# Sample attention of a hybrid layer: plain fp32 in four column groups of TensorE, two sequences at a time

## The chip, the cores and the metric

One core of a Trainium2 chip runs the program. The metric is the device time of one execution in microseconds (us); the time of the kernel before is the median of three runs.

## The reference, cut to what matters

One layer of a decoder is computed for a prompt of 1024 tokens and for 8 sample sequences of 8 new tokens each, which share all weights. The part that the change touches is the attention of the samples. Each sequence has 1024 past tokens in 8 pages of 128, picked by `page_table` from a pool of 80 pages, plus its own 8 new tokens; there are 8 heads of 64.

```python
def fox_attend(q, k, v, cq, ck, qpos, kpos):
    s = jnp.einsum('bqhd,bkhd->bhqk', q, k).astype(jnp.float32) * ATT_SCALE
    s = s + jnp.swapaxes(cq, 1, 2)[..., None] - jnp.swapaxes(ck, 1, 2)[:, :, None, :]
    mask = kpos[None, :] <= qpos[:, None]
    p = jax.nn.softmax(jnp.where(mask, s, -jnp.inf), axis=-1)
    return jnp.einsum('bhqk,bkhd->bqhd', p.astype(v.dtype), v)

def fox_sample(q, k, v, logf, k_past, v_past, logf_past, pos):
    k_all = jnp.concatenate([k_past.astype(k.dtype), k], axis=1)
    v_all = jnp.concatenate([v_past.astype(v.dtype), v], axis=1)
    c_all = jnp.cumsum(jnp.concatenate([logf_past, logf], axis=1), axis=1)
    ...
```

## The kernel before, in words

All 1088 tokens (1024 of the prompt, then 64 of the samples) go through the projections together, transposed, 128 channels at a time. The kernel keeps fp32 accuracy in two ways. Most matmuls split each operand into a high part in fp32r and a rest (`wh`, `wl`, `hh`, `hl`), and take three matmuls (`mm3`, L171). A few are plain fp32 (the tiles `py`, `ph` and `pi` of the state-space stage, L735, L725 and L755): the trace shows each of those as two TensorE records.

The stages follow each other: normalisation, pooling, prompt attention, the state-space scan, sample attention, then the output projections. In each stage `interleave` (L196) mixes the main work with side work, so that TensorE has something while the main work waits. The side work of the sample stage is 13 of the 24 merge gates (`gate_steps`, L217): a gate is 72 matmuls in 6 steps of 12, on weights that arrive in two halves (`raw<-w`, SP), are rounded by ScalarE (`wh`, L166) and subtracted by GpSimd (`wl`, L167). `issue_after` holds a gate step behind the main step that lies `LAG[3]` steps back. Within that, the scheduler of the tile framework fixes the order of every engine's queue at build time, the order of the DMA issues on SP among them.

The sample stage is L881 to L1064. `load_k` (L908) fetches the keys of one sequence in four tiles `kr` of two pages, `load_v` (L918) the values in eight tiles `vr` of one page. For each sequence `b`:

- `scores(b)` (L926): every key tile is rounded by ScalarE into `kh` (L943), and VectorE or GpSimd write the rest `kl` (L944). The queries stand in `QB` as high and low parts. For each of four head pairs one matmul takes 128 columns of the array (high and low queries, both heads) with `kh`, and one takes 64 columns with `kl`. All four head pairs add into the same PSUM rows; high and low rows are added later.
- `softmax(b)` (L966) adds the decay row `ck`, takes the minimum, exponentiates into `T` (64 rows: 8 heads by 8 queries) and scales.
- `values(b)` (L1001): `T` is transposed in 8 pieces and split (`PT`), the values are split like the keys (`vh` L997, `vl` L998), and each page takes a matmul of 128 columns with `vh` and one of 64 columns with `vl`, each on all 512 value channels. Four transposes of `ol` pick out each head's own channels.

`samples` (L1045) runs `scores(0)`, `softmax(0)`, `scores(1)` and then, for each `b`, `values(b)` with `softmax(b + 1)` and `scores(b + 2)` mixed in. After the stage come the last three gates (L1066) and the output projections, all on TensorE.

Of the kernel before, what the change touches and what calls it, by code (L numbers as in the profile page):

```python
# [8 lines left out]
F = mybir.dt.float32  # L9
# [13 lines left out]
LAG = (99, 99, 40, 60)  # L23
# [4 lines left out]
def _tiles():  # L28
# [28 lines left out]
C_ID, C_M30, C_CBM, C_EL, C_CBS, C_ELS, C_INV, C_MB, C_MB7, C_CA8, C_SGN, C_MT, C_N = (  # L57
    0, 128, 256, 384, 512, 576, 640, 704, 712, 720, 728, 730, 734)


def kernel_body(ctx, tc, d):
# [65 lines left out]
    vsm = const.tile([64, 4, 128], F, name="vsm")  # L127
# [21 lines left out]
    lfD = dt_([8, NT], "lfD")  # L149
    ckD = dt_([64, 1032], "ckD")  # L150
    ckqD = dt_([8, 8, 8, 1032], "ckqD")
# [133 lines left out]
    def fd_chain():  # L285
# [40 lines left out]
        SP.dma_start(out=lfD, in_=e[0:8, :])  # L326
# [50 lines left out]
        for b in range(8):  # L377
            SP.dma_start(out=lg[b * 8:b * 8 + 8, 1024:1032], in_=lfD[:, 1024 + b * 8:1032 + b * 8])
# [5 lines left out]
        SP.dma_start(out=ckqD, in_=ckD.rearrange("(b h o) s -> b h o s", b=8, o=1).to_broadcast([8, 8, 8, 1032]))  # L384
# [59 lines left out]
    with ExitStack() as px:  # L444
# [101 lines left out]
        def vz(j):  # L546
# [5 lines left out]
            def v_done():  # L552
                SP.dma_start(out=d["o_v"][j], in_=vf)
                for i0 in (0, 4):
                    ps = psa()
                    for i in range(4):
                        PE.transpose(ps[:, i * 128:(i + 1) * 128], vf[:, (i0 + i) * 128:(i0 + i + 1) * 128], ident)
                    pv = ps.rearrange("p (i e x) -> p i e x", i=4, e=2)
                    S.copy(VS[:, i0:i0 + 4, :, 0:64], pv)
                    V.tensor_tensor(VS[:, i0:i0 + 4, :, 64:128], pv, VS[:, i0:i0 + 4, :, 0:64].bitcast(F), op=SUB)  # L560
                ps = psa()
                PE.transpose(ps[0:64, 0:128], vf[:, 1024:1088], ident)
                V.tensor_copy(vsm[:, j, :], ps[0:64, 0:128])
# [316 lines left out]

    with ExitStack() as px:  # L881
        a1 = px.enter_context(tc.tile_pool(name="a1", bufs=1))
        a2 = px.enter_context(tc.tile_pool(name="a2", bufs=2))
        a3 = px.enter_context(tc.tile_pool(name="a3", bufs=3))
        a4 = px.enter_context(tc.tile_pool(name="a4", bufs=4))
        a5 = px.enter_context(tc.tile_pool(name="a5", bufs=5))
        QB = [a1.tile([128, 576], R, name=f"QB{x}") for x in range(2)]
        Pn = [a1.tile([64, 64], F, name=f"Pn{x}") for x in range(2)]
        for x in range(2):
            V.memset(QB[x].bitcast(F), 0.0)  # L890
        ysm = a1.tile([128, 4, 64], F, name="ysm")
        vnh = a1.tile([64, 512], R, name="vnh")
        vnl = a1.tile([64, 512], R, name="vnl")
        vflat = vsm.rearrange("p j x -> p (j x)")
        S.copy(vnh, vflat)
        V.tensor_tensor(vnl, vflat, vnh.bitcast(F), op=SUB)
        knh = a1.tile([128, 4, 64], R, name="knh")
        knl = a1.tile([128, 4, 64], R, name="knl")
        S.copy(knh, ksm)
        V.tensor_tensor(knl, ksm, knh.bitcast(F), op=SUB)  # L900
        pages, kraw, vraw, score, soft = {}, {}, {}, {}, {}

        def page_of(b, p):
            if (b, p) not in pages:
                pages[b, p] = page(b, p)
            return pages[b, p]

        def load_k():  # L908

            for b in range(8):  # L910
                for u in range(4):
                    kraw[b, u] = kr = a5.tile([128, 4, 256], F, tag="kr", name="kr")
                    for p in range(2):
                        page_dma(out=kr[:, :, p * 128:p * 128 + 128],
                                 in_=d["ck"][bass.ds(page_of(b, 2 * u + p), 1)].rearrange("o p c s -> (o p) c s"))
                    yield

        def load_v():  # L918

            for b in range(8):  # L920
                for p in range(8):
                    vraw[b, p] = vr = a4.tile([128, 512], F, tag="vr", name="vr")
                    page_dma(out=vr, in_=d["cv"][bass.ds(page_of(b, p), 1)].rearrange("o s x -> (o s) x"))
                    yield

        def scores(b):  # L926

            bs = slice(b * 8, b * 8 + 8)
            qb = QB[b % 2]
            qv = qb.rearrange("p (h x) -> p h x", x=144)  # L930
            for e in range(2):
                p = slice(64 * e, 64 * e + 64)
                S.copy(qv[p, :, 8 * e:8 * e + 8], qsm[p, :, bs])
                V.tensor_tensor(qv[p, :, 64 + 8 * e:72 + 8 * e], qsm[p, :, bs],
                                qv[p, :, 8 * e:8 * e + 8].bitcast(F), op=SUB)
            pss = score[b] = [psa(f"s{n}") for n in range(3)]

            def split(u):
                keys(1)
                kr = kraw.pop((b, u))  # L940
# [4 lines left out]
                return kh, kl  # L945

            def products(ps, kh, kl):
# [6 lines left out]
            ahead = [split(0)]  # L954
            yield
            ahead.append(split(1))
            products(pss[2][:, 0:8], knh[:, :, bs], knl[:, :, bs])
            yield
            for u in range(4):
                kh, kl = ahead.pop(0)  # L960
                products(pss[u // 2][:, u % 2 * 256:u % 2 * 256 + 256], kh, kl)
                if u < 2:
                    ahead.append(split(u + 2))
                yield

        def softmax(b):  # L966

            bs = slice(b * 8, b * 8 + 8)
            pss, pn = score.pop(b), Pn[b % 2]
            ck = a1.tile([64, 1032], F, tag="ck", name="ck")  # L970
            SP.dma_start(out=ck, in_=ckqD[b].rearrange("h q s -> (h q) s"))
            V.tensor_tensor(ck[:, 1024:1032], ck[:, 1024:1032], cst[0:64, C_CA8:C_CA8 + 8], op=ADD)
            T = a2.tile([64, 1032], F, tag="T", name="T")
            mn = a2.tile([64, 4], F, tag="mn", name="mn")
            for n in range(3):
                w = 512 if n < 2 else 8
                sl = slice(n * 512, n * 512 + w)
                V.tensor_tensor(ck[:, sl], ck[:, sl], pss[n][64:128, 0:w], op=ADD)
                V.tensor_tensor_reduce(out=T[:, sl], in0=pss[n][0:64, 0:w], in1=ck[:, sl], scale=1.0,
# [8 lines left out]
            V.tensor_copy(pn[:, bs], T[:, 1024:1032])  # L988
            soft[b] = T, pn
            yield  # L990

        def split_v(b, p):
            next(vload, None)
            vr = vraw.pop((b, p))
            vh = a3.tile([128, 512], R, tag="vh", name="vh")
            vl = a3.tile([128, 512], R, tag="vl", name="vl")
            S.copy(vh, vr)  # L997
            (G if p % 2 else V).tensor_tensor(vl, vr, vh.bitcast(F), op=SUB)  # L998
            return vh, vl

        def values(b):  # L1001

            bs = slice(b * 8, b * 8 + 8)
            T, pn = soft.pop(b)
            PT = a2.tile([128, 8, 128], R, tag="PT", name="PT")
            PTn = a1.tile([64, 128], R, tag="PTn", name="PTn")
            ps = psa()
            for p in range(8):
                PE.transpose(ps[:, p * 64:p * 64 + 64], T[:, p * 128:p * 128 + 128], ident[0:64, 0:64])
            pv = ps.rearrange("p (c x) -> p c x", x=64)  # L1010
            S.copy(PT[:, :, 0:64], pv)
            V.tensor_tensor(PT[:, :, 64:128], pv, PT[:, :, 0:64].bitcast(F), op=SUB)  # L1012
            ps = psa()
            PE.transpose(ps[0:64, 0:64], pn, ident[0:64, 0:64])
            S.copy(PTn[:, 0:64], ps[0:64, 0:64])
            V.tensor_tensor(PTn[:, 64:128], ps[0:64, 0:64], PTn[:, 0:64].bitcast(F), op=SUB)
            ahead = [split_v(b, 0), split_v(b, 1)]
            yield
            po = psa("po")
            for p in range(8):  # L1020
                vh, vl = ahead.pop(0)
                if p < 6:
                    ahead.append(split_v(b, p + 2))
                PE.matmul(out=po, lhsT=PT[:, p, :], rhs=vh, start=(p == 0), stop=False)
                PE.matmul(out=po[0:64], lhsT=PT[:, p, 0:64], rhs=vl, start=False, stop=False)
                yield
            PE.matmul(out=po[0:64], lhsT=PTn[:, 0:64], rhs=vnl, start=False, stop=False)
            PE.matmul(out=po, lhsT=PTn, rhs=vnh, start=False, stop=True)
# [267 lines left out]
```

## Time and profile before

| | |
|---|---|
| runs | 1471.38, 1471.22 and 1466.72 us; median 1471.22 |
| profiled execution | 1468.5 us, span 1466.7 us |
| TensorE | matmul busy 96% of the span, weight loads 91% |
| VectorE, ScalarE, GpSimd | busy 53%, 42%, 37% |
| mean granted clock of TensorE | 0.985 |
| sample stage, first to last matmul | 885.7 to 1132.5 us of the span |

Times inside the execution are microseconds from the start of the span. A group of instructions is read as line, engine, operation, and output<-inputs; its shape is that of the moving operand, and 128*64 before it means 128 rows by 64 columns of the array. Matmuls are pipelined, so what one costs in a stream is the distance between two starts and not its duration.

### The profile page before, as it was taken

To read this page: it belongs to the slowest core of one execution; us is meant where nothing else is said; L and a number is where in the kernel's file an instruction comes from. 1 tells how busy PE (TensorE), PEld (TensorE's weight loads), DVE (VectorE), ACT (ScalarE), POOL (GpSimd) and SP (SyncE) were. 2 spreads that over 40 slices of the span, in tenths; PEclk is the share of its full clock that TensorE was granted. 3 is DMA by queue.
4 is the path that set the end of the run, shared out by engine and by line. 5 is a ranking of instruction groups with operands and counts; after the bars stand their busy time and mean duration, and the time that the engine had idled before them with its cause. 6 is when DMAs were issued, how large, how long until landed. Compare 5 with 4: busy or idle time off the path is not lost. (4 is left out here: it accounts for less than half of the span.)

```text
span 1466.7 us, 23303 instructions
## 1 busy us (share of the span) xinstructions
PE 1415.3 (96%) x8564; PEld 1331.3 (91%) x8564; DVE 775.6 (53%) x1436; ACT 616.3 (42%) x1292; POOL 541.1 (37%) x438
## 2 busy tenths in 40 slices
PE   6999999999999999999989899899999999999997
PEld 6999999999899999988888798889999999999786
DVE  7575368236526725649936834766531583233423
ACT  6221355355535525575554624455543521122411
POOL 3233232222223122226656644546543353354300
PEclk9999999999999999999999999899999999999999
DMA  6124312412321231249975948768753886432331
GB/s 211 43 74 141 107 52 74 140 52 69 125 81 67 83 119 57 95 140 315 278 245 158 271 150 237 213 204 250 219 192 122 301 298 214 164 123 80 124 120 65
DMA packets 168936, 222.57 MB, mean 152 GB/s; under 512 B 16741, under 2 KB 107063, under 8 KB 168823
## 3 DMA queue, kind: packets, MB, share of 16 engines
q1 hardware_dynamic: 168566, 220.83, 47.6%
q8 instruction: 67, 1.10, 0.3%
q14 instruction: 47, 0.38, 0.1%
q0 software_dynamic: 256, 0.26, 0.1%
HBM read 163.98 MB, written 59.18 MB: 152 GB/s over the span
## 5 line engine op out<-in xcount | busy, mean ns | idle before, releaser
L71 PE MATMUL g<-hh,wh 128*128 128x384 f32 (+1 forms) x1632 | 540.8, 333 | 4.7 <-ACT gt L226 1.9
L71 PE MATMUL g<-hl,wh 128*128 128x384 f32 (+1 forms) x1632 | 540.6, 331 | 1.5 <-DVE hl L280 1.5
L71 PE MATMUL g<-hh,wl 128*128 128x384 f32 (+1 forms) x1632 | 540.8, 332 | 0.0
L167 POOL TENSOR_TENSOR wl<-raw,wh 128x512 fp32r<-128x512 f32 x168 | 235.4, 1402 | 466.4 <-ACT wh L166 452.4
L71 PEld LDWEIGHTS g<-hh,wh 128*128 128x128 f32 x1632 | 309.9, 190 | 12.1 <-DVE z L214 2.7
L71 PEld LDWEIGHTS g<-hl,wh 128*128 128x128 f32 x1632 | 310.3, 190 | 7.7 <-DVE hl L280 2.0
L71 PEld LDWEIGHTS g<-hh,wl 128*128 128x128 f32 x1632 | 310.0, 190 | 3.7 <-issue 0.5
L166 ACT CAST wh<-raw 128x512 fp32r<-128x512 f32 x168 | 103.9, 619 | 261.6 <-PE g L71 157.4
L586 POOL TENSOR_TENSOR ckd<-ckb,cst 128x128 f32<-128x128 f32 x64 | 36.0, 567 | 127.1 <-DVE mn L600 101.2
L626 ACT CAST Ph<-pa 128x512 fp32r<-128x512 f32 (+1 forms) x96 | 45.0, 480 | 72.3 <-PE pa L75 63.0
L627 DVE TENSOR_TENSOR Pl<-pa,Ph 128x512 fp32r<-128x512 f32 (+1 forms) x96 | 52.1, 553 | 39.0 <-ACT Ph L626 28.0
L71 PE MATMUL g<-yh,wh 128*128 128x384 f32 (+1 forms) x192 | 63.3, 330 | 0.2 <-DVE ld L1106 0.2
L71 PE MATMUL g<-yl,wh 128*128 128x384 f32 (+1 forms) x192 | 63.1, 329 | 0.0
L71 PE MATMUL g<-yh,wl 128*128 128x384 f32 (+1 forms) x192 | 63.1, 329 | 0.0
L71 PE MATMUL g<-ch,wl 128*128 128x384 f32 (+1 forms) x192 | 62.7, 327 | 0.0
L71 PE MATMUL g<-cl,wh 128*128 128x384 f32 (+1 forms) x192 | 62.6, 326 | 0.0
L71 PE MATMUL g<-ch,wh 128*128 128x384 f32 (+1 forms) x192 | 62.6, 326 | 0.0
L998 POOL TENSOR_TENSOR vl<-vr,vh 128x512 fp32r<-128x512 f32 x32 | 46.1, 1451 | 38.5 <-ACT vh L997 29.1
L604 ACT ACTIVATE T<-T,mn 128x128 f32<-128x128 f32 (+3 forms) x64 | 49.7, 777 | 21.6 <-DVE mn L600 20.8
L697 ACT ACTIVATE E<-E,cumN 128x128 f32<-128x128 f32 (+1 forms) x144 | 43.3, 383 | 29.4 <-DMA E<-cumD 29.3
L75 PE MATMUL pa<-cst,T 128*128 128x128 f32 (+1 forms) x352 | 53.5, 264 | 0.2 <-DVE T L986 0.2
L600 DVE CUSTOM_DVE_ANT_0 T<-pa,ckb 128x512 f32<-128x512 f32 (+3 forms) x56 | 31.8, 574 | 40.4 <-PE pa L71 39.5
(302 smaller groups left out, 2547.8 us busy)
## 6 DMA issues: line engine op xcount, KB each, us to landing
raw<-w SPq DMA_DIRECT2D x168, 256.0 KB
kr<-ck SPq DMA_DIRECT2D x64, 256.0 KB
vr<-cv SPq DMA_DIRECT2D x64, 256.0 KB
gD<-gt SPq DMA_DIRECT2D x24, 544.0 KB
ld<-gD SPq DMA_DIRECT2D x24, 544.0 KB
E<-cumD SPq DMA_DIRECT2D x16, 512.0 KB
xdD<-cth SPq DMA_DIRECT2D x8, 544.0 KB
zcD<-z SPq DMA_DIRECT2D x8, 544.0 KB
```

What stands on the lines that cost most here:

```text
L71: last["pe"] = nc.tensor.matmul(**kw)
L75: last["pe"] = nc.tensor.transpose(*args)
L166: S.copy(wh, raw)
L167: G.tensor_tensor(wl, raw, wh.bitcast(F), op=SUB)
L586: G.tensor_tensor(ckd, ckb[e][:, i * 128:n], cst[:, C_M30:C_M30 + 128], op=ADD)
L600: V.tensor_tensor_reduce(out=T[:, x0:x1], in0=ps[:, x0 - s0:x1 - s0], in1=in1, scale=1.0, scalar=cur, op0=ADD, op1=MIN, accum_out=mn[:, e, ...
L604: S.activation(T[:, 0:n], T[:, 0:n], AF.Exp, scale=-1.0, bias=cur, accum_out=l[:, e, i:i + 1])
L626: S.copy(Ph[:, q0:512], ps[:, q0:512])
L627: V.tensor_tensor(Pl[:, q0:512], ps[:, q0:512], Ph[:, q0:512].bitcast(F), op=SUB)
L697: S.activation(E[0:nt, h, 0:nt], E[0:nt, h, 0:nt], AF.Relu, scale=-1.0, bias=cumN[0:nt, c, r0 + h:r0 + h + 1])
L998: (G if p % 2 else V).tensor_tensor(vl, vr, vh.bitcast(F), op=SUB)
```

## The change

Two sequences (`2m` and `2m + 1`) are treated together, so that there are four rounds of scores, softmax and values where there were eight. Keys, values, queries and softmax weights stay in plain fp32: `kh`, `kl`, `vh`, `vl` and the other parts are gone. The queries stand in `QB` with, for each sequence and head pair, 32 columns: 2 heads by 2 sequences by 8 queries, of which the other sequence's are zero. Each head pair's matmul uses 32 columns of the array and writes its own 32 PSUM rows, so that four head pairs fill the 128 columns and rows. The values go the same way: each head pair multiplies only its own 128 channels. Softmax rows are ordered by head pair, head, sequence, query (128 rows), and the tables that feed them (`lfD`, `ckqD`, `ptr`, `hcol`, `C_CA8`) are laid out to match; a mask column `C_BB` separates the two sequences where new tokens meet. The key ring has 6 tiles where there were 5, the value ring 8 where there were 4, and both are now released by TensorE. `LAG[3]` falls from 60 to 30 steps, for 90 steps of main work where there were 191.

```diff
-LAG = (99, 99, 40, 60)
+LAG = (99, 99, 40, 30)
...
-    vsm = const.tile([64, 4, 128], F, name="vsm")
+    vsm = const.tile([128, 4, 128], F, name="vsm")
+    G.memset(vsm, 0.0)
...
-        a3 = px.enter_context(tc.tile_pool(name="a3", bufs=3))
-        a4 = px.enter_context(tc.tile_pool(name="a4", bufs=4))
-        a5 = px.enter_context(tc.tile_pool(name="a5", bufs=5))
-        QB = [a1.tile([128, 576], R, name=f"QB{x}") for x in range(2)]
+        ak = px.enter_context(tc.tile_pool(name="ak", bufs=6))
+        av = px.enter_context(tc.tile_pool(name="av", bufs=8))
+        QB = a1.tile([128, 8, 4, 40], F, name="QB")
...
-            for b in range(8):
+            for m in range(4):
                 for u in range(4):
-                    kraw[b, u] = kr = a5.tile([128, 4, 256], F, tag="kr", name="kr")
+                    for b in (2 * m, 2 * m + 1):
+                        kr = ak.tile([128, 4, 256], F, tag="kr", name="kr")
...
-                kh = a2.tile([128, 4, 256], R, tag="kh", name="kh")
-                kl = a2.tile([128, 4, 256], R, tag="kl", name="kl")
-                S.copy(kh, kr)
-                (G if u % 2 else V).tensor_tensor(kl, kr, kh.bitcast(F), op=SUB)
...
-                    two = [(128, kh), (64, kl)]
-                    for m_, x in two if hp < 3 else two[::-1]:
-                        PE.matmul(out=ps[0:m_], lhsT=qb[:, hp * 128:hp * 128 + m_], rhs=x[:, hp],
-                                  start=(hp == 0 and m_ == 128), stop=(hp == 3 and m_ == 128))
+                    o = 8 - 8 * bb
+                    PE.matmul(out=ps[32 * hp:32 * hp + 32], lhsT=QB[:, 2 * m + bb, hp, o:o + 32], rhs=x[:, hp],
+                              start=(bb == 0), stop=(bb == 1))
...
-                PE.matmul(out=po, lhsT=PT[:, p, :], rhs=vh, start=(p == 0), stop=False)
-                PE.matmul(out=po[0:64], lhsT=PT[:, p, 0:64], rhs=vl, start=False, stop=False)
...
+            def products(bb, lhs, x, first, last):
+                for hp in range(4):
+                    r = slice(32 * hp, 32 * hp + 32)
+                    PE.matmul(out=po[r, 128 * bb:128 * bb + 128], lhsT=lhs[:, r], rhs=x[:, hp * 128:hp * 128 + 128],
+                              start=first, stop=last)
...
-        interleave(samples(), 191, gate_steps(SHARE[2]), 6 * SHARE[2], LAG[3])
+        interleave(samples(), 90, gate_steps(SHARE[2]), 6 * SHARE[2], LAG[3])
```

How the change moves instructions is shown at three places. In the rows `g` is a gate's matmul, and the shape is the columns of the array by the moving elements.

First place, TensorE at the first scores. Before:

```order
L71 MATMUL g<-hh,wh 128x320
L71 MATMUL s_9503<-kl,QB_9400 64x256
L71 MATMUL s_9503<-kh,QB_9400 128x256
...
L71 MATMUL s_9503<-kl,QB_9400 64x256 x2
L71 MATMUL s_9503<-kh,QB_9400 128x256 x2
L71 MATMUL g<-hl,wh 128x320
```

Of the change, the same place:

```order
L71 MATMUL g<-hh,wl 128x320
L71 MATMUL s_9505<-ksm,QB 32x8 x8
L71 MATMUL s_9503<-kr,QB 32x256 x12
L71 MATMUL g<-hh,wh 128x320
L71 MATMUL g<-hl,wh 128x320
...
L71 MATMUL s_9503<-kr,QB 32x256 x4
...
L71 MATMUL s_9504<-kr,QB 32x256 x4
```

Where one key tile was eight fp32r matmuls of 128 and 64 columns, it is now four plain ones of 32 columns, and the first three tiles stand together without a gate between them. Over the whole stage the 32-column matmuls (128 with `kr`, 32 with `ksm`, 256 with `vr`, 32 with `vsm`) form 56 blocks with gate matmuls or transposes between them.

Second place, TensorE at the values. Before (here mixed with the scores of a later sequence):

```order
L71 MATMUL g<-hh,wh 128x384
L71 MATMUL po<-vh,PT 128x512
L71 MATMUL g<-hl,wh 128x384
L71 MATMUL g<-hh,wl 128x384
...
L71 MATMUL s_11219<-kh,QB_9401 128x256 x2
L71 MATMUL po<-vl,PT 64x512
L71 MATMUL po<-vh,PT 128x512
L71 MATMUL g<-hl,wh 128x384
```

Of the change:

```order
L71 MATMUL g<-hh,wh 128x384
L71 MATMUL g<-hl,wh 128x384
L71 MATMUL po<-vr,PT 32x128 x8
L71 MATMUL g<-hh,wl 128x384
...
L71 MATMUL po<-vr,PT 32x128 x8
L71 MATMUL g<-hh,wh 128x384
...
L71 MATMUL s_11282<-ksm,QB 32x8 x8
```

Two pages of values are one block of eight 32-column matmuls now, mostly with 12 gate matmuls to the next block, where single matmuls of 128 and 64 columns stood between gates before.

Third place, the DMA queue SP near the start of the stage, with each tile's number; a key tile has two such rows, one for each of its pages, of which one is shown. Before, three halves of gate weights and the second `ck` row go out between the key tiles of the third sequence:

```order
L99 DMA kr_9763<-ck 128x4x128
...
L163 DMA raw_10244<-w 128x512
L163 DMA raw_10468<-w 128x512
L163 DMA raw_10474<-w 128x512
L971 DMA ck_9934<-ckqD_152 64x1032
...
L99 DMA kr_9804<-ck 128x4x128
...
L99 DMA kr_9837<-ck 128x4x128
...
L99 DMA vr_9922<-cv 128x512
```

Of the change (the first row is a page of the twelfth key tile, 9781 is the thirteenth, 9986 the fourteenth):

```order
L99 DMA kr_9756<-ck 128x4x128
...
L99 DMA kr_9781<-ck 128x4x128
...
L99 DMA vr_9885<-cv 128x512
...
L99 DMA vr_9951<-cv 128x512
...
L99 DMA kr_9986<-ck 128x4x128
...
L164 DMA raw_10054<-w 128x512
L164 DMA raw_10060<-w 128x512
...
L99 DMA kr_10025<-ck 128x4x128
```

After the first 14 key tiles (28 pages) and seven pages of values come the next two halves of gate weights; none goes out between the first key page and them. A key page that takes the place of an earlier tile waits until TensorE has used that tile, where it waited for the engines that split it before.

## Rows read from the trace of the kernel before

**Rows 1.** The page, part 1 (busy time of TensorE, share of the span, instructions) and the clock line of part 2: one digit for each of 40 equal slices, in tenths of full clock.

```profile
PE 1415.3 (96%) x8564; PEld 1331.3 (91%) x8564; DVE 775.6 (53%) x1436; ACT 616.3 (42%) x1292; POOL 541.1 (37%) x438
...
PEclk9999999999999999999999999899999999999999
```

**Rows 2.** Busy time by stretches, from the first sample matmul (885.7) to the last (1132.5) and on: length, then busy us of PE, PEld, DVE, ACT and POOL with their instructions, the granted clock, the share of the DMA engines and GB/s.

```profile
885.70:917.00 31.30, 27.84 (x194) 26.56 (x192) 13.86 (x19) 15.70 (x24) 15.04 (x8) 1.00 0.92 269
917.00:924.00 7.00, 5.63 (x19) 5.51 (x20) 5.36 (x11) 1.91 (x5) 2.50 (x2) 0.51 0.90 283
941.00:944.40 3.40, 3.33 (x14) 3.33 (x15) 3.37 (x7) 1.45 (x2) 1.15 (x1) 0.52 1.15 320
944.40:1132.50 188.10, 187.75 (x1176) 171.44 (x1174) 92.79 (x160) 94.42 (x169) 92.61 (x59) 1.00 0.65 199
1132.50:1180.00 47.50, 47.50 (x288) 47.24 (x287) 25.35 (x24) 20.92 (x29) 15.72 (x10) 1.00 0.85 289
```

**Rows 3.** Groups of TensorE's matmuls by form between 885.7 and 1132.5: line, engine, operation, out<-in, rows*columns of the array, moving operand, count | busy us, mean ns of one | idle before them and what ended it.

```profile
L71 PE MATMUL g<-hl,wh 128*128 128x384 f32 x203 | 69.8, 344 | 0.0
...
L71 PE MATMUL s<-kh,QB 128*128 128x256 f32 x128 | 33.8, 287 | 1.4 <-ACT kh L943 1.4
L71 PE MATMUL g<-hl,wh 128*128 128x320 f32 x104 | 32.6, 314 | 0.0
...
L71 PE MATMUL s<-kl,QB 128*64 128x256 f32 x128 | 28.5, 285 | 3.6 <-DVE kl L944 3.3 <-POOL kl L944 0.3
L71 PE MATMUL po<-vh,PT 128*128 128x512 f32 x64 | 25.5, 399 | 0.4 <-DVE PT L1012 0.3
...
L71 PE MATMUL s<-knh,QB 128*128 128x8 f32 x32 | 5.9, 231 | 0.0
L75 PE MATMUL pa<-cst,T 64*128 64x64 f32 x64 | 5.3, 224 | 0.2 <-DVE T L986 0.2
...
L71 PE MATMUL po<-vnl,PTn 64*64 64x512 f32 x8 | 3.5, 443 | 0.0
...
```

**Rows 4.** TensorE's timeline in the sample stage: start us, duration us, line, operation, out<-in, columns of the array, moving operand, count. The distance of two starts is what one matmul costs in a stream.

```profile
960.66 0.39 PE L71 MATMUL po<-vl,PT 128*64 128x512 f32 x1
...
961.59 0.39 PE L71 MATMUL po<-vl,PT 128*64 128x512 f32 x1
...
961.84 0.20 PE L71 MATMUL s<-knl,QB 128*64 128x8 f32 x1
961.90 0.25 PE L71 MATMUL s<-knh,QB 128*128 128x8 f32 x1
962.01 0.20 PE L71 MATMUL s<-knl,QB 128*64 128x8 f32 x1
...
962.61 0.28 PE L71 MATMUL s<-kl,QB 128*64 128x256 f32 x1
...
963.31 0.28 PE L71 MATMUL s<-kh,QB 128*128 128x256 f32 x1
```

**Rows 5.** The same view in the state-space stage before it: three gate matmuls, a block of plain fp32 matmuls into 64 columns of the array each (8 in the program, at alternating column halves, two records each), then plain fp32 matmuls over all 128 columns (4 in the program, 8 records).

```profile
698.14 0.33 PE L71 MATMUL g<-hh,wh 128*128 128x384 f32 x1
698.32 0.34 PE L71 MATMUL g<-hl,wh 128*128 128x384 f32 x1
698.59 1.09 PE L71 MATMUL py<-E,xdt 128*64 128x128 f32 x16
699.61 1.16 PE L71 MATMUL pi<-CT,hst 128*128 128x128 f32 x8
700.61 1.02 PE L71 MATMUL ph<-xw,Bn 128*128 128x512 f32 x2
```

**Rows 6.** All records of those column-half matmuls (shortest, median, longest duration in ns; first and last start).

```profile
L71 PE MATMUL py<-E,xdt x288: 218/273/366, 674.5 to 832.9; 128*64 128x128 f32 x128, 64*64 64x64 f32 x16
```

**Rows 7.** The timeline again: such a block whose moving operand has 64 elements and 64 rows, 16 records.

```profile
832.47 0.68 PE L71 MATMUL py<-E,xdt 64*64 64x64 f32 x16 [1.13 <-DVE E L710]
```

**Rows 8.** The timeline: 64-row transposes of the weights T of one sequence, and what follows them.

```profile
1083.42 0.71 PE L75 MATMUL pa<-cst,T 64*128 64x64 f32 x8
1083.97 0.22 PE L75 MATMUL pa<-cst,Pn 64*64 64x64 f32 x1
```

**Rows 9.** Who TensorE waited for between 885 and 1133 (us in total, times, longest).

```profile
PE s L71 <- DVE kl L944: 3.3, 1, 3.3
PE pa L75 <- DVE Pn L988: 3.0, 1, 3.0
PE s L71 <- ACT kh L943: 1.4, 1, 1.4
```

**Rows 10.** The DMA queue SP from 880 to 912: start us, time over which the issues stretch, DMA, count.

```profile
880.32 0.46 SPq L828 DMA_DIRECT2D rsD<-rst  x1
883.46 0.64 SPq L99 DMA_DIRECT2D kr<-ck  x1
...
884.96 13.62 SPq L99 DMA_DIRECT2D kr<-ck  x13
```

**Rows 11.** Groups of ScalarE's instructions between 885.7 and 1132.5 (columns as in rows 3).

```profile
L943 ACT CAST kh<-kr 128x1024 fp32r<-128x1024 f32 x32 | 33.4, 1048 | 41.9 <-PE s L71 25.5 <-DMA kr<-ck 8.8 <-issue 6.4
```

**Rows 12.** The chain that ended last, in order of time: start us, us, engine and line.

```profile
1132.29 0.39 PE pa L75 x4
1132.68 45.96 PE g L71 x276
```

More of the change, by code (lines that the diff above doesn't have):

```diff
@@ L958, in scores @@
             yield
             for u in range(4):
[L960 to L974, printed above, removed]
+                for bb in range(2):
+                    next(kload, None)
+                    products(pss[u // 2][:, u % 2 * 256:u % 2 * 256 + 256], bb, kraw.pop(0))
+                    yield
@@ L987, in softmax @@
             V.memset(pn, 0.0)
-            V.tensor_copy(pn[:, bs], T[:, 1024:1032])
-            soft[b] = T, pn
+            for bb in range(2):
+                o = 16 * m + 8 * bb
+                V.tensor_scalar(pn[:, o:o + 8], T[:, 1024:1032], cst[:, C_BB + bb:C_BB + bb + 1], None, op0=MUL)
+            soft[m] = T, pn
             yield
[L992 to L1006, printed above, removed]
-            ps = psa()
[L1008 to L1017, printed above, removed]
+        def values(m):
+            T, pn = soft.pop(m)
+            PT = a2.tile([128, 8, 128], F, tag="PT", name="PT")
+            PTn = a2.tile([128, 128], F, tag="PTn", name="PTn")
+            for c in (0, 4):
+                ps = psa()
+                for p in range(4):
+                    PE.transpose(ps[:, p * 128:p * 128 + 128], T[:, (c + p) * 128:(c + p) * 128 + 128], ident)
+                S.copy(PT[:, c:c + 4, :], ps.rearrange("p (c x) -> p c x", x=128))
+            ps = psa()
+            PE.transpose(ps[:, 0:128], pn, ident)
+            V.tensor_copy(PTn, ps[:, 0:128])
@@ L1029, in values @@
[L1029 to L1031 removed]
+            def products(bb, lhs, x, first, last):
[3 more added lines that the diff above has]
+                              start=first, stop=last)
+            for bb in range(2):
+                for p in range(8):
+                    next(vload, None)
+                    products(bb, PT[:, p, :], vraw.pop(0), p == 0, False)
+                    if p == 7:
+                        products(bb, PTn, vsm.rearrange("p j x -> p (j x)"), False, True)
+                    if p % 2:
+                        yield
@@ L1045, in samples @@
+            yield
         def samples():
-            keys(4)
+            for _ in range(5):
+                next(kload)
             yield from scores(0)
             yield from softmax(0)
-            next(vload)
-            next(vload)
+            for _ in range(7):
+                next(vload)
             yield from scores(1)
-            for b in range(8):
-                v = values(b)
-                m = softmax(b + 1) if b < 7 else iter(())
-                k = scores(b + 2) if b < 6 else iter(())
-                for x in (v, m, v, m, v, m, v, v, k, v, k, v, k, v, k, v, k, v, k, v, v, m):
-                    next(x, None)
-                    yield
+            for m in range(4):
+                v = values(m)
+                s = softmax(m + 1) if m < 3 else iter(())
+                k = scores(m + 2) if m < 2 else iter(())
+                for x in (s, v, s, v, s, v, k, v, k, v, k, v, k, v, k, v, k, v, k, v, k, v, k, v):
+                    if next(x, "end") != "end":
+                        yield
```

127 lines of the change are left out of this document (52 added, 75 removed).

## The prediction

> **What bounds the kernel now.** I read the busy times first: TensorE's matmuls cover 96% of the span, at nearly full clock throughout [rows 1]. Then the stretches of the sample stage: from 944.4 to its end at 1132.5 TensorE is busy without a break, but before that it is busy for 27.8 of 31.3 us up to 917.0 and for 5.6 of the next 7.0, and in two stretches, of 7.0 and 3.4 us, the granted clock is at half, 1.2 of 2.4 GHz [rows 2]; at the start of each stands a wait of about 3 us, for `Pn` and for `kl` [rows 9]. Behind the stage TensorE is busy at once for 46 us of gate matmuls [rows 2, 12]. So the stage is worth what TensorE needs for its matmuls, plus its early idle time; no other engine sets its end.
>
> How the stage's 246.8 us are made up I take from counts and from distances of starts. Gate matmuls: three forms of 203 with 384 elements at 0.173 (698.14 to 698.32 gives 0.18, and such a stream 0.173 on average), and some 311 with 320 elements at 0.147, by the ratio of the sizes [rows 3, 5]: 609 x 0.173 + 311 x 0.147 = 151.1 us. Scores: 256 matmuls [rows 3] at (963.31 - 962.61) / 6 = 0.117 [rows 4]: 30.0. Values: 64 with `vh` [rows 3] and as many with `vl`, at (961.59 - 960.66) / 4 = 0.232 [rows 4]: 29.8. New keys: 32 pairs [rows 3] at 962.01 - 961.84 = 0.17 [rows 4]: 5.4. New values: 16, of longer duration than the others [rows 3], for which I estimate 0.3: 4.8. Transposes of 64 rows: 13 a sequence, 104, at (1083.97 - 1083.42) / 8 = 0.069 [rows 8]: 7.2. The sample work sums to **77.2 us**, everything to 228.3; the other 18.5 us are waits (7.7 of them named: a split of keys that was late, and the first weights `Pn`) [rows 9], half clock (10.4 us at half speed, at most 5.2 lost) [rows 2], and small change.
>
> **The price of a narrow fp32 matmul.** The new form, 32 columns in plain fp32, does not occur. Its neighbour does: a block of 8 plain matmuls into alternating halves of 64 columns, two records each. From 698.59 to 699.61 the 16 records take 1.02 us, and the 8 full-width records behind them take 1.00 us, from 699.61 to 700.61 [rows 5]. So a full-width record costs 0.125 with its edges, a half-width one 0.064: two column groups run at the same time, each at its full speed. Inside the block, without the edges, 15 starts lie in 1.09 - 0.27 = 0.82 us (the last record's duration, 0.27, is the median [rows 6]), 0.055 each or 0.109 a round of two. A record with 256 elements then takes 0.218 a round.
>
> How many of four groups run at once, no row shows. The bounds are two, the most that is seen, and four, if each group goes on its own as the two did. I take **four**: the two lose nothing to each other, and the 16 records of a small block start 0.031 us apart, (0.68 - 0.22) / 15 [rows 6, 7], so TensorE can issue a load and a record in about the 0.027 that four at once would ask for. The Trainium skill speaks more cautiously: its page "TensorE: Matmul & The Clock Gate", section "Measured speedup vs the span model", gives 2.38 times for three column tiles. An estimate by that page is 2.38 / 3 x 4 = 3.2 at once, and by it the sum below would come out about 7 us longer; no run here shows it yet.
>
> **The change, part by part.** With four at once:
> - scores: 128 matmuls, 256 records, 256 x 0.218 / 4 = 14.0 us;
> - values: 256 matmuls, 512 records, 512 x 0.109 / 4 = 14.0; new values 64 records: 1.7;
> - new keys: 64 records of 8 elements at the smallest distance seen, 0.031 [rows 7]: 2.0;
> - transposes: 32 of `T`, 4 of `Pn`, 8 of `ol`, now 128 rows wide, at about twice 0.069, less the fixed part, say 0.115: 5.0;
> - edges: before and behind a block TensorE loses time. From the last gate start to the start behind the block are 699.61 - 698.32 = 1.29 us [rows 5]; a gate step of 0.173 and 8 rounds of 0.109 are 1.05, so 0.24 a block. 56 blocks: 13.4.
>
> Sum **50.1 us** against 77.2: TensorE saves 27.1 us, all of it on the path. The other engines' work is a gain only where TensorE waited for it. ScalarE loses its 32 roundings of keys [rows 11] and 64 of values, VectorE and GpSimd the subtractions; of that only the key waits of rows 9 (4.7) were on the path. The first wait for `Pn` (3.0) goes too, since the scores of the second pair now stand between the first softmax and its transposes. What comes late next are the loads: TensorE eats the keys faster, and the next two halves of gate weights stand on SP behind 28 key pages and seven of values. Of the 18.5 us I therefore take only 6 as gained, between none and all. The smaller edits are free: one DMA in place of eight for the new decay values, and a memset of `vsm`, lie in stages where SP and GpSimd have slack and TensorE does not wait for them; the wider softmax rows cost VectorE and ScalarE no more per instruction and halve their count. The shorter `LAG[3]` is already in the order that the blocks were counted from.
>
> 1468.5 - 27.1 - 6 = 1435.4 us for the profiled execution. That execution is 2.7 below the median of the runs; I put the forecast for a median between the two references, at **1437 us**.
>
> **The rivals.**
> 1. *The loads bind early.* In the first stretch the DMA engines are 0.92 busy at 269 GB/s [rows 2], and 13 key pages take 13.6 us to go out, 1.05 each [rows 10]. The 35 pages ahead of the gate weights are 37 us, more with the rows and gate results between them. The first key page now precedes `rsD` on SP, behind which it stood at 883.46 [rows 10]; if that brings it to about 872, the weights arrive near 911, if not, near 922. TensorE wants them after some 116 gate matmuls, 12 tiles and 8 block edges, 27 us behind 885.7, at 913. So it waits 0 to 10 us. I have about 2 of that in the sum; the worst end adds 8, or 12 with a stretch of half clock: 1445 to 1449.
> 2. *Two at a time.* If four column groups share what two use up, the 29.7 us of streams become 59.4; with 20.4 for the rest that is 79.8, 2.6 above before, less the 6 of waits. 1468.5 - 3.4 + 1.6 = 1467. For it: two is all that is seen. Against: no sign of a loss at two.
> 3. *Slower: fewer than two.* With R groups at once the sample work is 118.8 / R + 20.4. It crosses 77.2 + 6 at R = 1.9; below that the edges of 56 blocks and the doubled records turn the change into a loss. If the four groups with operands from four places end up one after another, R = 1: 139.2 us, 56 more than before net of waits, 1526 us. Against it stands the column-half block [rows 5], where R is 2.
> 4. *Weight loads don't hide.* Each narrow record needs its own load. A load of 64 columns paces small matmuls at 0.06 (961.84 to 961.90) [rows 4], so one of 32 columns about 0.03; if the four of a round were paid ahead of it, 208 rounds x 0.12 = 25 us come on top: 1462. In the column-half block a round of 0.109 has two loads of 64 columns, 0.12, beside its records [rows 5, 6], so they must overlap there. The Trainium skill has the rule for this rival: the same page, section "The mechanism", says that a load overlaps matmuls in flight only when their row groups differ, and here all groups use all rows. By that rule the time is this rival's; the trace of the column halves disagrees with it.
>
> **How the numbers follow.** Forecast 0.59, loads 0.11, two at a time 0.19, weight loads 0.04, slower 0.07. The range has all waits gone at its low end, 1437 - 12.5 = 1424, and at its high end reaches to just under two at a time, 1466; what lies outside is the slower rival and most of "two at a time", about 0.2. A measurement tells 0.3%, 4.4 us, from no change: faster is below 1466.8. Two at a time lies on that edge, and I split it 0.08 faster, 0.07 same, 0.04 slower. Faster 0.59 + 0.11 + 0.04 + 0.08 = 0.82, same 0.07, slower 0.07 + 0.04 = 0.11.
>
> **What the changed profile would show.** If right: records of `s<-kr` in groups of four starts, a tile of 8 records in about 0.44 us and a value block of 16 in about 0.44 without edges; a last sample matmul near 1100 in place of 1132.5; hardly a wait of TensorE for anything but a key page or `wl` early on; the same 330 us behind the stage. Two at a time would show 0.87 for both, the load rival a gap before the gate matmuls some 27 us into the stage with GpSimd's `wl` at its end, the weight-load rival starts of narrow loads 0.03 apart that the records wait for. The forecast is wrong if the last sample matmul comes after 1120.

## The result, and the profile after

The changed kernel takes 1436.01 us, the median of four runs (1432.96 to 1438.14); the kernel before took 1469.56 beside it. The ratio is 0.977 (95% interval 0.975 to 0.980): 33.55 us faster. The forecast was 1437. The profiled execution took 1438.14 us with a span of 1436.4, against 1468.5 and 1466.7.

The page's line of busy times, which answers to [rows 1]:

```profile
PE 1381.2 (96%) x8936; PEld 1282.0 (89%) x8936; DVE 668.1 (47%) x1285; ACT 537.4 (37%) x1160; POOL 449.6 (31%) x391
```

TensorE is as full as before and 34 us less busy, with 372 more records. VectorE, ScalarE and GpSimd lost 79 to 108 us each, the splits of keys, values and weights; the program is 30 us shorter, so most of that was off the path.

The stretches of the sample stage, now from 889.39 to 1100.53 (columns as in [rows 2]):

```profile
889.39:917.00 27.61, 27.36 (x246) 21.92 (x246) 3.14 (x11) 4.26 (x8) 1.29 (x1) 1.00 0.86 259
917.00:921.20 4.20, 0.56 (x3) 0.16 (x2) 0.00 (x0) 0.81 (x2) 0.14 (x1) 1.00 0.83 254
921.20:924.80 3.60, 3.60 (x15) 2.35 (x16) 0.00 (x0) 0.76 (x2) 2.37 (x2) 0.53 0.89 277
924.80:1100.53 175.73, 174.71 (x1589) 150.08 (x1588) 12.80 (x51) 36.96 (x73) 28.19 (x22) 1.00 0.72 225
```

The stage lasts 211.1 us where it lasted 246.8. One hole is left, at 917, with a short stretch of half clock behind it. Behind the stage TensorE is busy at once, as before: for all of the 47.47 us up to 1148. Who TensorE waited for in the stage, in answer to [rows 9] (us in total, times, longest):

```profile
PE g L71 <- ACT wh L167: 4.2, 2, 3.6
PE g L71 <- POOL wl L168: 0.4, 1, 0.4
```

Every wait of rows 9 is gone and a new one has come: a gate matmul that waits for its weights (in this kernel `wh` is L167 and `wl` L168). The queue SP shows why (in answer to [rows 10]):

```profile
874.98 10.35 SPq L99 DMA_DIRECT2D kr<-ck  x12
...
894.08 11.31 SPq L99 DMA_DIRECT2D kr<-ck  x12
...
907.25 1.54 SPq L99 DMA_DIRECT2D kr<-ck  x2
908.98 3.65 SPq L99 DMA_DIRECT2D vr<-cv  x7
913.20 1.29 SPq L99 DMA_DIRECT2D kr<-ck  x2
914.60 1.04 SPq L164 DMA_DIRECT2D raw<-w  x2
```

The weights leave at 914.60, behind 28 key pages in all (12, 12, 2 and 2) and seven of values; TensorE has run out of gate work at 917.4 and goes on at 921.0.

The trace has 256 records of `s<-kr` and 512 of `po<-vr`, as the prediction counted. TensorE's timeline around one key tile, the new keys of two sequences, and one block of two value pages (columns as in [rows 4, 5]):

```profile
895.20 0.34 PE L71 MATMUL g<-hh,wl 128*128 128x384 f32 x1
895.47 0.64 PE L71 MATMUL s<-kr,QB 128*32 128x256 f32 x8
896.04 0.45 PE L71 MATMUL g<-hh,wh 128*128 128x384 f32 x1
896.32 0.34 PE L71 MATMUL g<-hl,wh 128*128 128x384 f32 x1
...
951.87 0.34 PE L71 MATMUL g<-hh,wl 128*128 128x384 f32 x1
952.14 0.31 PE L71 MATMUL s<-ksm,QB 128*32 128x8 f32 x16
952.38 0.41 PE L71 MATMUL g<-hh,wh 128*128 128x320 f32 x1
952.63 0.30 PE L71 MATMUL g<-hl,wh 128*128 128x320 f32 x1
...
954.09 0.31 PE L71 MATMUL g<-hh,wl 128*128 128x320 f32 x1
954.33 0.65 PE L71 MATMUL po<-vr,PT 128*32 128x128 f32 x16
954.90 0.44 PE L71 MATMUL g<-hh,wh 128*128 128x384 f32 x1
955.18 0.33 PE L71 MATMUL g<-hl,wh 128*128 128x384 f32 x1
```

How to read these: a block's cost is a distance of starts, and it must reach to the second gate matmul behind it. For the key tile 895.20 to 896.32 is 1.12 us; two gate steps of 0.173 off, 0.774 is left. (A gate step here is the distance of two gate matmuls in a stream, 0.173 for 384 elements and 0.147 for 320.) Its 8 records at four at once are two rounds of 0.218, 0.436. So 0.338 is edge, time that the block costs beside its rounds: 0.10 ahead of the block (895.20 to 895.47 is 0.27 where a gate step is 0.173), some 0.13 in and behind it, and 0.11 where nobody looks, between the first and the second gate start behind it (896.04 to 896.32 is 0.28). The value block gives the same: 954.09 to 955.18 less 0.147 and 0.173 is 0.77, less four rounds of 0.109 it is 0.33. Over all blocks of one kind at full clock these distances repeat within 0.006 us, so I use **0.34 us a block**.

### The profile page after: what moved, and what is told of

Its sections match the earlier page's. It is cut to its first block, busy times and chain, and to the rows that moved or that the text cites. A ratio compares the mean times of both kernels' runs of the same rounds, so it can differ in the third digit from the quotient of the medians.

```text
span 1436.4 us, 23728 instructions
## 1 busy us (share of the span) xinstructions
PE 1381.2 (96%) x8936; PEld 1282.0 (89%) x8936; DVE 668.1 (47%) x1285; ACT 537.4 (37%) x1160; POOL 449.6 (31%) x391
## 5 line engine op out<-in xcount | busy, mean ns | idle before, releaser
L168 POOL TENSOR_TENSOR wl<-raw,wh 128x512 fp32r<-128x512 f32 x168 | 231.1, 1377 | 587.4 <-ACT wh L167 497.7
L167 ACT CAST wh<-raw 128x512 fp32r<-128x512 f32 x168 | 103.9, 619 | 332.3 <-PE g L71 171.9
L227 ACT ACTIVATE gt<-g 128x384 f32<-128x384 f32 (+1 forms) x72 | 33.8, 469 | 85.2 <-PE g L71 85.1
L75 PE MATMUL pa<-cst,T 128*128 128x128 f32 x320 | 52.3, 272 | 0.0
L71 PE MATMUL o<-wol,mh 128*128 128x512 f32 x128 | 50.8, 401 | 0.9 <-DVE wol L1104 0.9
```

The costliest lines, as they stand in the source:

```text
L71: last["pe"] = nc.tensor.matmul(**kw)
L75: last["pe"] = nc.tensor.transpose(*args)
L167: S.copy(wh, raw)
L168: G.tensor_tensor(wl, raw, wh.bitcast(F), op=SUB)
L227: S.activation(gt[:, a:b], ps, AF.Tanh, scale=0.5)
```

## The experiments

All times are medians beside runs of the kernel before on the same chip; the ratios are to it, with 95% intervals. The first run is the changed kernel again.

**The yardstick.** No edit.

> The changed kernel itself, unedited, as the yardstick for the others on this chip. Every theory expects 1433 to 1438 us, a ratio of 0.975 to 0.980 to the kernel before.

1435.78 us, ratio 0.977 (0.975 to 0.979). In its profile the stage takes 211.4 us, with waits of 5.2. Runs of one kernel lie up to 7 us apart, so the small effects below are read inside the stage.

**Four groups at once or not.** The value products at full width:

```diff
-                    PE.matmul(out=po[r, 128 * bb:128 * bb + 128], lhsT=lhs[:, r], rhs=x[:, hp * 128:hp * 128 + 128],
-                              start=first, stop=last)
+                    PE.matmul(out=po[:, 128 * bb:128 * bb + 128], lhsT=lhs, rhs=x[:, hp * 128:hp * 128 + 128],
+                              start=first and hp == 0, stop=last and hp == 3)
```

> The changed kernel with the value products at full width: each of the four matmuls of a page takes all 128 columns of PT, and all four add into the same 128 rows of PSUM, so the head pairs are not kept apart; number of matmuls, moving operands and loads stay. Theory A, four column groups run at the same time: a page goes from 0.22 to 8 records x 0.109 = 0.87 us, 64 pages and 8 of new values are 47 us more; 26 fewer entries into the 32-column form give up to 8.6 back if the edges belong to it. 1474 to 1483 us. Rival B, the products were not what saved the time (the splits and waits that went did): within 10 us of 1436.

1476.37 us, ratio 1.006 (1.004 to 1.008): 40 us more than the changed kernel, and slower than the kernel before. The scores kept their column groups. Two value pages in its timeline:

```profile
955.92 0.31 PE L71 MATMUL g<-hh,wl 128*128 128x320 f32 x1
956.07 1.95 PE L71 MATMUL po<-vr,PT 128*128 128x128 f32 x16
957.77 0.42 PE L71 MATMUL g<-hh,wh 128*128 128x384 f32 x1
958.03 0.34 PE L71 MATMUL g<-hl,wh 128*128 128x384 f32 x1
```

955.92 to 958.03, less 0.147 and 0.173, is 1.79 us for 16 records: 0.112 each, and nothing is left for an edge. So plain fp32 at full width has no edges; the 0.34 belongs to the 32-column form. And a page costs 0.89 at full width against 0.218 in four groups: four at once, whole. With the values alone out of their column groups the program is slower than the kernel before: without the groups there is no gain. That settles theory A against rival B.

**Does the order of the four matter?** Two pages head pair by head pair:

```diff
-                    products(bb, PT[:, p, :], vraw.pop(0), p == 0, False)
+                    if p % 2:
+                        two = [vraw.pop(0), vraw.pop(0)]
+                        for hp in range(4):
+                            r = slice(32 * hp, 32 * hp + 32)
+                            for y in range(2):
+                                PE.matmul(out=po[r, 128 * bb:128 * bb + 128], lhsT=PT[:, p - 1 + y, r],
+                                          rhs=two[y][:, hp * 128:hp * 128 + 128], start=(p + y == 1), stop=False)
```

> The changed kernel with the two pages of a value block taken head pair by head pair: both pages' matmuls of one column group stand together, four records in a row on the same group, where the groups took turns after each matmul. Theory A, TensorE starts records strictly in program order and a record waits for the group's last one: a block goes from 4 rounds to about 13, from 0.44 to 1.4 us, 32 blocks are 31 us: 1467 us. Theory B, each column group works on its own behind a common stream of instructions, so that the order within 16 records does not matter: 1436 us, starts in fours as before.

1436.01 us, ratio 0.978 (0.977 to 0.980). The block in its timeline:

```profile
952.39 0.67 PE L71 MATMUL po<-vr,PT 128*32 128x128 f32 x16
952.99 0.45 PE L71 MATMUL g<-hh,wh 128*128 128x384 f32 x1
```

0.60 from the block's start to the gate behind it, against 0.57. Theory A (strict order, 1.4 us) falls: within 16 records a column group does not hold up the others.

**What an edge is worth.** Larger blocks, values by four pages and scores by two tiles (35 blocks in the order):

```diff
-LAG = (99, 99, 40, 30)
+LAG = (99, 99, 40, 20)
...
                     products(pss[u // 2][:, u % 2 * 256:u % 2 * 256 + 256], bb, kraw.pop(0))
-                    yield
+                yield
...
-                    if p % 2:
+                    if p % 4 == 3:
                         yield
...
-        interleave(samples(), 90, gate_steps(SHARE[2]), 6 * SHARE[2], LAG[3])
+        interleave(samples(), 58, gate_steps(SHARE[2]), 6 * SHARE[2], LAG[3])
```

> The changed kernel with values in blocks of four pages and scores in blocks of two key tiles: 35 blocks of 32-column matmuls in TensorE's order in place of 56, the same records. Theory A, read from the trace of the changed kernel: a block costs 0.33 us of edges (0.095 ahead, 0.13 in and behind it, and 0.106 more at the second gate matmul behind it, which the prediction's 0.24 left out): 21 blocks less are 7.0 us, 1429 us. By the prediction's 0.24 they are 5.0 us, 1431 us. Rival B, the loss goes with the records or with the wait for gate weights and not with the edges: 1435 to 1437, no change. Rival C, larger blocks eat keys faster than the loads bring them, a wait for kr in place of the edges: 1436 or more.

1434.6 us, ratio 0.976 (0.974 to 0.978), not to be told from the yardstick. A block of two key tiles, and the waits in the stage:

```profile
970.00 0.31 PE L71 MATMUL g<-hh,wl 128*128 128x320 f32 x1
970.24 1.07 PE L71 MATMUL s<-kr,QB 128*32 128x256 f32 x16
971.25 0.44 PE L71 MATMUL g<-hh,wh 128*128 128x384 f32 x1
971.53 0.34 PE L71 MATMUL g<-hl,wh 128*128 128x384 f32 x1
```

```profile
PE g L71 <- ACT wh L167: 4.7, 2, 4.4
PE po L71 <- DMA vr<-cv: 2.1, 4, 1.3
PE s L71 <- DMA kr<-ck: 1.4, 1, 1.4
```

970.00 to 971.53 less two gate steps is 1.21 us; one tile took 0.774, so the second costs 0.436, two clean rounds, and one edge is saved. 21 blocks less should give 7.1; waits of 8.2 in place of 5.2 take 3.0 of it, which leaves 4.1, and the stage is 3.1 shorter (208.3). The total lies between the ranges and decides nothing; the block bears out theory A on the edge, and the new waits rival C on what comes next.

Then values by eight pages and scores by four tiles (28 blocks); the lines are against the run just above:

```diff
-LAG = (99, 99, 40, 20)
+LAG = (99, 99, 40, 15)
...
-                yield
+                if u % 2:
+                    yield
...
-                    if p % 4 == 3:
+                    if p == 7:
...
-        interleave(samples(), 58, gate_steps(SHARE[2]), 6 * SHARE[2], LAG[3])
+        interleave(samples(), 42, gate_steps(SHARE[2]), 6 * SHARE[2], LAG[3])
```

> The same with values in blocks of eight pages and scores in blocks of four key tiles: 28 blocks, and one half of gate weights now goes out on SP ahead of the later key pages. Theory A: 28 blocks less at 0.33 are 9.2 us, and up to 4 of the wait for gate weights with it: 1423 to 1427. By 0.24: 1426 to 1430. Rival B (edges cost nothing): only the wait, 1432 to 1436. Rival C (loads): a block of eight pages waits for vr or a block of four tiles for kr, some us for each of the first blocks: 1432 or more.

1442.21 us, ratio 0.981 (0.979 to 0.983): slower than the yardstick. Its waits:

```profile
PE s L71 <- DMA kr<-ck: 5.7, 4, 2.5
PE po L71 <- DMA vr<-cv: 5.3, 6, 3.1
PE pa L75 <- DVE mn L950: 3.9, 1, 3.9
```

28 blocks less are 9.5 us; against them stand 9.7 more of waits and 20.5 us at half clock in the stage (3.5, 6.8 and 10.2) where the yardstick has 3.5, of which at most half is lost. The stage is 7.3 longer (218.7). Rival C: the larger blocks wait for their loads, 11.0 us of the 14.9; the other 3.9 are for `mn` of the softmax.

**The hole at 917.** Fewer value pages ahead, so that weights leave earlier:

```diff
-            for _ in range(7):
+            for _ in range(2):
                 next(vload)
```

> The changed kernel with two value pages fetched ahead of the values where there were seven; by it the next half of gate weights goes out on SP ahead of 14 key pages and not behind them. Theory A, the wait of 3.6 us at 917 is for weights that stand behind pages on SP: it goes, and the stretch of half clock behind it (some 1.5 us), 1431 us. Rival B, the DMA engines are full there (0.99 busy from 900 to 920), so an earlier weight makes a key page later: TensorE waits for kr instead, 1434 to 1438.

1436.07 us, ratio 0.978 (0.976 to 0.980). The waits in the stage:

```profile
PE po L71 <- DMA vr<-cv: 3.6, 2, 2.6
PE s L71 <- DMA kr<-ck: 1.4, 2, 1.1
```

The wait for weights is gone, and as long a one for pages has taken its place: rival B, though more of it is for values than for the keys that it named.

The rings of the kernel before:

```diff
-        ak = px.enter_context(tc.tile_pool(name="ak", bufs=6))
-        av = px.enter_context(tc.tile_pool(name="av", bufs=8))
+        ak = px.enter_context(tc.tile_pool(name="ak", bufs=5))
+        av = px.enter_context(tc.tile_pool(name="av", bufs=4))
...
-            for _ in range(5):
+            for _ in range(4):
                 next(kload)
...
-            for _ in range(7):
+            for _ in range(3):
                 next(vload)
```

> The changed kernel with the rings of the kernel before: five key tiles and four value tiles, four and three of them fetched ahead. Theory A, the stage stands at the edge of its loads (taking five value pages out of the way of the weights only moved the wait to vr and kr): smaller rings bring TensorE waits for vr and kr of 5 to 20 us in all, 1440 to 1455 us. Rival B, the rings are long enough as they were, only the order on SP matters: 1432 to 1438 us.

1435.87 us, ratio 0.980 (0.977 to 0.982). Theory A expected 1440 to 1455 and was wrong; rival B (1432 to 1438) holds. There is one kind of wait above 0.5 us, again of the same size:

```profile
PE po L71 <- DMA vr<-cv: 5.0, 5, 3.9
```

The longer rings of the change bought nothing that shows in the time; inside, the stage is 2.0 us longer than the yardstick's (213.4).

A longer key ring:

```diff
-        ak = px.enter_context(tc.tile_pool(name="ak", bufs=6))
+        ak = px.enter_context(tc.tile_pool(name="ak", bufs=10))
...
-            for _ in range(5):
+            for _ in range(9):
                 next(kload)
```

> The changed kernel with ten key tiles in the ring where there were six, nine of them fetched ahead. The first key pages then need not wait for TensorE to free a tile (the pause from 885.3 to 894.1 on SP). Theory A, the pause is what makes the loads late: the waits of 4.6 us go, half clock with them, 1429 to 1432 us. Rival B, the order on SP decides: the gate weights now stand behind 34 or more key pages without a break, TensorE waits for wh as long or longer: 1436 to 1445 us.

1452.23 us, ratio 0.990 (0.988 to 0.992): half of the gain lost by more buffers, and above the ranges of both theories. SP (columns as above) now sends 30 key pages in one row, but from 883.72, where the first left at 874.98, and the next weights only at 936.69:

```profile
883.72 31.85 SPq L99 DMA_DIRECT2D kr<-ck  x30
...
936.69 0.56 SPq L164 DMA_DIRECT2D raw<-w  x1
```

TensorE's waits in the stage:

```profile
PE s L71 <- DMA kr<-ck: 8.9, 5, 2.4
PE g L71 <- ACT wh L167: 5.3, 2, 5.1
PE po L71 <- DMA vr<-cv: 4.0, 5, 1.5
```

Rival B has the direction: the wait for `wh` is as long as it was or longer, and the order on SP became worse. But two things moved at once. The first key page now stands behind `rsD`, which it preceded in the changed kernel, and the waits for `kr` are new. So the run shows that this order costs; what the pause alone costs it does not show.

**More time for the loads.** Two more gates in the stage:

```diff
-SHARE = (6, 2, 13)
+SHARE = (6, 2, 15)
```

> The changed kernel with 15 gates mixed into the sample stage in place of 13, so that one is left behind it. The stage gets 25 us more of gate work between the same loads, and TensorE's order has 66 blocks of 32-column matmuls in place of 56. Theory A, edges 0.34 us a block and loads that come too late by some us only because the samples ask for them too fast: +3.4 for the edges, -4 to -7 for the waits of TensorE and the half clock behind them: 1432 to 1436 us. Rival B, the waits come from the order on SP alone: they stay, 1438 to 1440 us.

1443.27 us, ratio 0.985 (0.982 to 0.987). That is above the ranges of both theories. Inside the stage theory A holds: TensorE is busy for 230.39 of 230.53 us, at full clock. But the last gate is followed by the matmuls of the output projections on `yh`, and these, 96.7 us long in the changed kernel, take 109.2. The stretch of these matmuls in the changed kernel (columns as in [rows 2]):

```profile
1136.50:1233.20 96.70, 96.48 (x578) 95.93 (x578) 52.54 (x71) 18.37 (x25) 43.13 (x28) 1.00 0.70 245
```

The stage of this kernel, and its stretch of the same matmuls:

```profile
886.95:1117.48 230.53, 230.39 (x1993) 195.75 (x1993) 18.02 (x62) 47.77 (x94) 37.81 (x29) 1.00 0.69 221
1129.30:1238.50 109.20, 100.92 (x580) 97.34 (x579) 62.02 (x79) 24.47 (x31) 46.34 (x29) 0.98 0.74 264
```

Its longest waits from the stage to the end of that stretch, all of them behind the stage:

```profile
PE g L71 <- DVE ld L1072: 3.8, 4, 1.6
PE g L71 <- ACT yh L1054: 3.0, 1, 3.0
```

So the gates left behind the stage had covered the loads of the projections; with two of them taken away, the wait stands there.

With the blocks of four pages and two tiles, the same edit, then 16 and 14 in the place of 15:

> The kernel with blocks of four value pages and two key tiles (35 blocks), and 15 gates in the stage in place of 13. Theory A: 21 blocks less are 7.1 us, and the loads have 25 us more time, so that the 8.2 us of waits for wh, vr and kr that the larger blocks showed fall below 3: 1424 to 1429 us. Rival B, the waits come from the order on SP and stay: 1432 to 1436 us.

1441.08 us, ratio 0.982 (0.980 to 0.984). Missed in the same way: the last gate matmul starts at 1121.9, 14 us earlier than in the changed kernel, and the matmuls on `yh` take 109.8. The profiled execution is the fastest of the five (1435.32), so it does not show what made the others slower.

> The same with all 16 gates in the stage, so that none is left behind it. Theory A: waits as small as with 15 or smaller, but the loads and roundings of yb after the last sample product have no gate to lie beside: 0 to 6 us of TensorE waiting there, 1424 to 1433 us. Rival B: 1432 to 1440 us.

1443.19 us, ratio 0.983 (0.981 to 0.986): one wait of 7.0 for `yh`, and 5.6 for `ld`.

> Blocks of four value pages and two key tiles (34 blocks in TensorE's order), and 14 gates in the stage, two left behind it. With 15 the waits inside the stage nearly went and came back behind it, as waits for yh, yl and ld where the loads of the output projections lost their cover. Theory A: with two gates left as cover, the waits behind the stage fall below 3 us, those inside stay below 6, and the 22 blocks less give 7.4 us: 1427 to 1432 us. Rival B, what the loads cost is only moved from the stage to the place behind it, whatever the number of gates: 1434 to 1440 us.

1441.67 us, ratio 0.982 (0.979 to 0.984). Missed: 7.6 for `wh` in the stage and 4.6 for `ld` behind it. All four of these runs lie above the ranges of both of their theories, by 1.7 to 5.1 us over rival B's. What the profiles bear out is the mechanism of the last rival B: the wait moves from the stage to the place behind it. No version here is measurably faster than the changed kernel.

## Why the prediction was right

The forecast of 1437 against 1436.0 is closer than its parts were. Its own steps, by the trace:

| us, in the sample stage | predicted | measured | from |
|---|---|---|---|
| scores | 14.0 | 14.0 | 32 tiles x 0.436 |
| values | 14.0 | 14.0 | 64 pages x 0.218 |
| new values | 1.7 | 1.7 | 8 x 0.218 |
| new keys | 2.0 | 0.4 | (0.76 - 0.32 - 0.34) = 0.10, four times |
| transposes | 5.0 | 4.8 | 44 x 0.11 |
| edges | 13.4 | 19.0 | 56 x 0.34 |
| sum | 50.1 | 53.9 | |
| gain against 77.2 | 27.1 | 23.3 | |
| waits, half clock, small change | 12.5 | 8.2 | 211.1 less 149.0 of gates and the sum |

- **Four at once** was right and complete: the full-width run gives the factor, 0.89 to 0.218. The Trainium skill, "TensorE: Matmul & The Clock Gate", section "Measured speedup vs the span model", has 2.38 times for three tiles. By it, as the prediction estimated, the sum would have been about 7 us longer; this trace shows 4.1 times for four. In the single records of the trace, which the rows above merge, the four starts of a round lie 7 ns apart, and a tile's second round starts 0.22 behind the last start of its first; two at a time would have shown 0.87 for a tile.
- **Weight loads hide.** A round has four loads of 32 columns, whether its records have 256 elements (0.218) or 128 (0.109): it goes with the elements, and nothing is left over for the loads. The Trainium skill, the same page, section "The mechanism", lets a load overlap matmuls in flight only where row groups differ. Here all 128 rows are shared, and the trace disagrees with it for column groups.
- **The edge was mis-sized**, 0.24 for 0.34, and so its term was 5.6 too low. The prediction ended its count at the first start behind the block and missed the 0.11 at the second. That 0.11 stood in its own rows: eight full-width records took 1.00 us [rows 5] and were read as 0.125 each; they cost 0.112, and the rest was the edge of the block ahead.
- **The waits** were mis-sized the other way: of 18.5 us, 6 were taken as gained and 10.3 were. Before, 7.7 us were named waits [rows 9] and 10.4 us ran at half clock [rows 2]; now 4.6 us are waits and 3.6 us run at half clock. Both old stretches of half clock began at waits that the change removes, and went with them. That makes 3.1 us of waits and at most 3.4 of half clock. The other 3.8 us or more are neither; the prediction had them as small change. A part of them were edges of the kernel before, around its 64-row transposes, here four of `ol`:

```profile
1080.11 0.34 PE L71 MATMUL g<-hl,wh 128*128 128x384 f32 x1
1080.37 0.46 PE L75 MATMUL pa<-cst,ol 64*128 64x64 f32 x4
...
1081.04 0.33 PE L71 MATMUL g<-hh,wh 128*128 128x384 f32 x1
```

  The 0.93 us from 1080.11 to 1081.04, less two gate steps of 0.173 and four transposes at the prediction's 0.069, leave 0.31. Nine such blocks come to some 2.4 us in the stage. Two of the 128-row transposes of the change:

```profile
987.64 0.31 PE L71 MATMUL g<-hh,wl 128*128 128x320 f32 x1
987.79 0.38 PE L75 MATMUL pa<-cst,ol 128*128 128x128 f32 x2
...
988.18 0.33 PE L71 MATMUL g<-hl,wh 128*128 128x384 f32 x1
```

  987.64 to 988.18 less gate steps of 0.147 and 0.173 is 0.22: 0.11 each, and no edge. So the prediction counted the edges of the new form and not those that went. Where the rest of the 3.8 us lay is not shown.
- **The loads** came as the rival said, in the right place: weights wanted 28 us into the stage (predicted: 27), and late there by 3.6. Between "0 to 10, about 2 in the sum" it was the lower half. The gap ended with ScalarE's `wh`, where the rival had named GpSimd's `wl`.
- **LAG[3]** did nothing: with 60 in its place the built program is the same, so every engine's order is.
- The sums: sample work 23.3, waits, half clock and small change 10.3, and 2.1 of gate matmuls, of which 12 more now stand behind the stage, make the 35.7 us by which the stage is shorter. The span is only 30.3 shorter (the profiled execution took 1438.14 where 1435.4 had been worked out for it), because the stage starts 3.7 later and what lies behind it is 1.7 longer (those 12 gate matmuls). The late start is in the state-space stage ahead, where TensorE waits 6.1 us for `ysum` against 2.4. In the profiles of the edits the stage starts anywhere from 884.4 to 889.4, and I could name no edit that goes with it: the cause stays open, and a forecast of this kernel from one execution is no better than these 4 us.

So the two errors cancelled: 3.8 less than predicted from the sample work, 4.3 more from the waits and the small change. The mechanism was right, and the agreement to 1 us was luck.

## What to carry to other kernels

Where an operand fills only a quarter of TensorE's columns, side by side in four column groups makes plain fp32 as cheap as one full-width pass over a quarter of the work. Most of the gain lies there; of the splits that fall away on other engines only what TensorE waited for counts, 4.7 us here [rows 9]. Count the blocks as well as the records, in the old kernel as in the new one, and measure an edge to the second start behind a block. Before making blocks larger, buffers deeper or cover thicker, ask which load is late next: here each such edit was paid back, in the stage or behind it, and none gained.

## What the runs showed of the hardware that was not expected

- Entering and leaving 32-column matmuls costs 0.34 us a block, whatever the block's length (one tile, two tiles, two pages). Plain fp32 at full width between the same gate matmuls costs none: 16 records in 1.79 us. The 64-row transposes of the kernel before cost as much, 0.31 for a block of four.
- The order within a block of 16 records hardly matters: with four records in a row on one column group it was only 0.03 us longer.
- 16 records of 8 elements cost 0.10 us beside an edge of 0.34, some 6 ns each, below the 0.031 seen for the same number in two groups [rows 7].
- In the stage of the run with 15 gates TensorE neither waits nor falls to half clock; where it waits for 3.6 us in the changed kernel, 3.6 us at a clock of 0.53 follow.
